# A hybrid decoder layer on one core: sums of weights spread over other blocks, small buffers lent out, state-space outputs one slot later

## The chip, the core and the metric

The kernel runs on one core of a Trainium2 chip. TensorE (PE) does the matrix products, VectorE (DVE) and ScalarE (ACT) the elementwise work, GpSimd (POOL) and SyncE (SP) mostly issue transfers (DMAs); POOL also does a few copies. The metric is device time of one execution in microseconds (us). A profile is one execution recorded by the hardware profiler; its times are its own and stand beside the median of unprofiled executions.

## The reference

One inference step of one decoder layer, for a prompt of 1024 positions and 8 sample rows (1032 tokens, width 1024), in float32:

```
z = x @ w_in + b_in                       # -> ssm input (512) | u, v (2 x 512) | gate_a (1024) | gate_b (1024)
y_a = S5 state-space mixer (32 groups of 16 channels, 64 complex states each), GELU, GLU with w_glu
y_b = u * (tril(W_s) LayerNorm(v) + b)    # in chunks of 128 positions
merged = sigmoid(gate_a) * (y_a @ w_branch_a) + sigmoid(gate_b) * (y_b @ w_branch_b)
x1 = LN1(alpha * x + merged @ w_out + b_out)
x2 = LN2(alpha * x1 + relu(x1 @ w_up + b_up)^2 @ w_down + b_down + sigmoid(x1 @ w_pg + b_pg) * (p @ w_ple))
```

Outputs are x2, the final S5 states and the normalised v rows of the samples.

## The kernel before

Activations lie with features on partitions and tokens in the free dimension. Every float32 product is made of three fast products: an operand is split into a high part (a rounded copy, on ScalarE or VectorE) and a low part (the operand less the high part, on VectorE), and TensorE adds high x high, high x low and low x high. `split` (line 105) makes both parts; a class `Stream` (line 150) loads weights into three `raw` tiles and splits them into four `hl` tiles, three blocks ahead. Line 86 (`tt`) and line 83 (`stt`) are the helpers through which nearly all VectorE operations go, so operations are told apart by their tiles.

The order of the work: input projection of the state-space part; 48 slots, in each of which one third of a gate column block is multiplied (24 matmuls, `gate_tile`), and in which the state-space part is placed by hand in a table (`at(slot, function, ...)`, lines 729 to 761); the v and u parts; the GLU; eight merge blocks of 72 matmuls (lines 999 to 1013); the output projection in two passes with LN1; the gate and embedding products (pg, ple); the up-projection in 16 pairs; the down-projection; LN2. A planner (the framework's) turns this program into one fixed instruction order for each engine and each DMA queue: it takes what its model holds for ready, earlier program text first. On the chip every engine and every queue then goes through its list in order and waits at each instruction for what that needs.

State-space part: `ssm_h` (line 648) makes the carried states H on VectorE with the powers er and ei, stored as (power, group); four transfers on SP's queue put H into the tile Hst. `ssm_y` (line 677) makes the outputs of 8 groups: two matmuls each, of which the second reads Hst, three evacuations on ScalarE into Y, and nine stores. `load_u` and `setup_dve` (lines 553 and 478) prepare the next groups.

The up- and down-projection use a scheme with seven products in place of eight (P1 to P7), so the down-projection needs sums of w_down blocks, S1 to S4. They are made ahead, in 16 sets: `sums_in` (line 933) loads four half tiles ds0 to ds3 (called dsum in the profile) on POOL's queue, `sums_out` (line 946) combines them on VectorE and stores four results on POOL's queue. In front of each load, a one-element copy on VectorE (line 942) writes into the tile from a value made at that point of the program, which ties the load to that moment; the copy itself can run only when the tile's last store has landed. One set is loaded at the end of the u part, two in the GLU, one in each of the eight merge blocks, one in the output projection, and the last four in the first pairs of the up-projection. Outside the sets ds0 serves LN1 and LN2, and ds1 the last normalisation.

The up-projection (`up_pair`, line 1302) takes one pair of 128 hidden columns after the other, 168 matmuls each. Its four `hl` tiles are made by `up_prep` (line 1273) from two weight rows: ra (in a raw tile) and rd (tile rawu in a unit, B18 for even pairs, B19 for odd). B18 and B19 hold parts of the ple operand until the ple products are over. The products P6, P7 and P4 add into the PSUM tile of P1, so each needs the evacuation of the one before it. Squared hidden rows hA and hB and their combinations tA and tB go to DRAM (hd) on POOL's queue; tA and tB have one buffer each.

The down-projection reads hidden rows back: `h_load` (line 1414) loads two of them into a row tile (hraw), of which there are four (`rtags`: B18, A8, A9, B19), and `h_prep`/`h_ahead` (lines 1422 and 1442) split them into 23 operand tiles (hop), each with a one-element copy in front that ties it to a product of the last pair. A8 and A9 are hA and hB of the pair before the last.

Of the kernel before, what the change touches and what calls it, by code (L numbers as in the profile page):

```python
# [32 lines left out]
HF = NTOK // 2  # L33
# [24 lines left out]
def hybrid_step_kernel(ctx: ExitStack, tc: tile.TileContext, i, o):  # L58
# [589 lines left out]
    def ssm_h(hf, gh):  # L648
        g8 = slice(8 * hf, 8 * hf + 8)
        Lv = lview(hf)  # L650
        C = Cc[hf]
        if gh == 0:
            stH[hf] = sp.tile([128, 2, 8, HC], F32, tag="H", name="H")
        H = stH[hf]
        Hv = H[:, :, :, 0:NCH].rearrange("p r g (s b) -> p r g s b", b=8)
        ht = tview(0, (4, 16, 8))
        gs = slice(4 * gh, 4 * gh + 4)
        ge = slice(8 * hf + 4 * gh, 8 * hf + 4 * gh + 4)
        shp = [128, 4, 16, 8]
        eb = lambda x: x[:, 0:8, ge].rearrange("p b g -> p g b").unsqueeze(2).to_broadcast(shp)  # L660
        cb = lambda ri: C[:, ri, gs, 0:16].unsqueeze(3).to_broadcast(shp)
        for ri in range(2):
            tt(V, Hv[:, ri, gs], eb(er), cb(ri), ALU.mult)
            tt(V, ht, eb(ei), cb(1 - ri), ALU.mult)
            tt(V, Hv[:, ri, gs], Hv[:, ri, gs], ht, ALU.subtract if ri == 0 else ALU.add)
            tt(V, Hv[:, ri, gs, :, 1:8], Hv[:, ri, gs, :, 1:8], Lv[:, ri, gs, :, 0:7], ALU.add)
        if gh == 0:
            P.tensor_copy(out=H[:, :, :, NCH:HC], in_=h0[:, :, g8, :])
        else:
            Hst = sp.tile([128, 16, HC], F32, tag="Sst", name="Hst")  # L670
            stS[hf] = Hst
            for ri in range(2):
                for g2 in range(2):
                    nc.sync.dma_start(out=Hst[64 * ri:64 * ri + 64, g2::2, :],
                                      in_=H[64 * g2:64 * g2 + 64, ri])
# [21 lines left out]
    setup_dve(0)  # L697

    carry_powers()
    for mp in range(2):  # L700
        up_ = sp.tile([128, 2, NTOK], F32, tag=["Sst", "L"][mp], name="uperm")
        for j in range(2):
            m = 2 * mp + j
            e = P if j else V
            e.tensor_copy(out=up_[:, j, 0:SEQ].rearrange("p (s n j) -> p s n j", s=8, n=8),
                          in_=ubuf[m][:, 0:SEQ].rearrange("p (n s j) -> p s n j", s=8, n=8))
            e.tensor_copy(out=up_[:, j, SEQ:NTOK], in_=ubuf[m][:, SEQ:NTOK])
            nc.sync.dma_start(out=ud[m], in_=up_[:, j, :])
# [32 lines left out]
    at(14, ssm_l3, 0)  # L741
    at(16, ssm_h, 0, 0)
    at(17, ssm_h, 0, 1)
    at(22, ssm_y, 0)
    at(22, load_u, 2)
    at(23, ssm_y, 1)
    at(23, load_u, 3)
    at(23, setup_dve, 2)
    at(26, setup_pe, 2)
    at(26, setup_dve, 3)  # L750
    at(28, ssm_S, 2)
# [5 lines left out]
    at(37, ssm_l3, 1)  # L757
    at(39, ssm_h, 1, 0)
    at(40, ssm_h, 1, 1)
    at(45, ssm_y, 2)  # L760
    at(46, ssm_y, 3)
    for slot in range(48):
        for f in plan.get(slot, []):
            f()
# [165 lines left out]
    quad = []  # L930
    nq = [0]

    def sums_in(after):

        if nq[0] == 16:
            return
        n = nq[0]
        mp, kh, g = n // 4, n // 2 % 2, n % 2
        nq[0] += 1
        ts_ = [bpool.tile([128, HF], F32, tag=f"ds{t}", name="dsum")[:, 0:512] for t in range(4)]  # L940
        for t, m, j in ((0, mp + 4, 0), (1, mp + 4, 1), (2, mp, 0), (3, mp, 1)):
            V.tensor_copy(out=ts_[t][:, 0:1], in_=after)  # L942
            dn_load(ts_[t], m, j, kh, (g,), nc.gpsimd)
        quad.append((n, ts_))

# [23 lines left out]
    for m in range(4):  # L969
        if m % 2 == 0:  # L970
            w = W("glu", m // 2)
        ps = mm_full([wsl(w, 4 * (m % 2) + k) for k in range(4)], yhl)
        sg = unit(f"T{m % 2}", name="sg")
        S.activation(out=f3(sg), in_=fv(ps), func=AF.Sigmoid, bias=col("b_glu", m))
        tt(V, sg, sg, yt[m], ALU.mult)
        a, b = unit(f"B{8 + m}", F32R, name=f"yah{m}"), unit(f"A{12 + m}", F32R, name=f"yal{m}")
        split(a, b, sg)
        ya.append((a, b))
        split(yb[m][0], yb[m][1], ubt[m])
        if m % 2:  # L980
            sums_out(sg[:, 0:1])
            sums_in(sg[:, 0:1])


    mtags = ["A8", "A9", "A10", "A11", "B0", "B1", "B2", "B3", "B4", "B5", "B6", "B7",
# [13 lines left out]
    for m in range(8):  # L999
        w = W("pab", m)  # L1000
        if m < 7:
            load_gate(m + 1)
        sa, sb = gl.pop(m)
        psB = mm_full([wsl(w, 4 + k) for k in range(4)], yb)
        tt(V, f3(sb), fv(psB), f3(sb), ALU.mult)
        psA = mm_full([wsl(w, k) for k in range(4)], ya)
        tt(V, f3(sa), fv(psA), f3(sa), ALU.mult)
        tt(V, sa, sa, sb, ALU.add)
        a, b = unit(mtags[2 * m], F32R, name=f"mgh{m}"), unit(mtags[2 * m + 1], F32R, name=f"mgl{m}")
        split(a, b, sa)  # L1010
        mg.append((a, b))
        sums_out(sa[:, 0:1])
        sums_in(sa[:, 0:1])

    half = lambda p_: slice(p_ * HF, (p_ + 1) * HF)
    quarter = lambda j: slice(j * QT, (j + 1) * QT)
# [153 lines left out]
    for j, (p_, m) in enumerate(passes):  # L1170
        w = W("out", p_, m)
        load_xr(j + 2)
        sl = half(p_)
        xr = xrs.pop(j)[:, 0:HF]
        S.activation(out=xr, in_=xr, func=AF.Identity, scale=ALPHA, bias=col("b_out", m))
        ps = region2()
        mm_half(ps, [wsl(w, k) for k in range(KD)], [(a[:, sl], b[:, sl]) for a, b in mg])
        tt(V, h2(pre[m][:, sl]), rv(ps), h2(xr), ALU.add)
        if m == 1:
            tt(V, ssum[:, sl], pre[0][:, sl], pre[1][:, sl], ALU.add)  # L1180
        elif m > 1:
            tt(V, ssum[:, sl], ssum[:, sl], pre[m][:, sl], ALU.add)
        if p_ == 0 and m == 7:
            lnx = bpool.tile([128, HF], F32, tag="ds0", name="lnx")
            lnq.add(ln_half(pre, 0, ssum, tmpu, lnx, "ln1_g", "ln1_b", x1_split))
        if p_ == 1:
            lnq.pull(1)
        elif m in (2, 5):
            sums_out(pre[m][:, 0:1])
            if m == 2:  # L1190
                sums_in(pre[m][:, 0:1])


    lnq.drain()
# [78 lines left out]
    def up_prep(n):  # L1273

        p, t = n // 4, n % 4
        if t == 0:
            ra, rb, rc = (raw_() for _ in range(3))
            rd = unit(free[8 + p % 2], F32, [128, 1024], name="rawu")
            upr[p] = (ra, rb, rc, rd)
            nc.sync.dma_start(out=ra, in_=i["w_up"][p])  # L1280
            nc.sync.dma_start(out=rd, in_=i["w_up"][p + NP])
        ra, rb, rc, rd = upr[p]
        if t == 1:
            tt(V, rb[:, D5], rd[:, C5], rd[:, D5], ALU.add)
            tt(V, rb[:, C5], rb[:, D5], ra[:, C5], ALU.subtract)
        elif t == 2:
            tt(V, rc[:, C5], ra[:, C5], rd[:, C5], ALU.subtract)
            tt(V, rc[:, D5], ra[:, D5], rb[:, C5], ALU.subtract)
        w = hl_()
        c = D5 if t == 3 else slice(0, 1024)  # L1290
        split(w[:, 0, c], w[:, 1, c], (ra, rb, rc, rd)[t][:, c])
        wq[n] = w

    def up_ahead(n):
# [7 lines left out]
    def up_pair(p):  # L1302
# [11 lines left out]
        ps = {"P1": a, "P6": a, "P7": a, "P4": a, "P5": c, "P3": c, "P2": b}  # L1314
        last = p == NP - 1
        if last:
            for n in range(4):
                h_load(n)
        for nm, t, cs_ in UPO:
            up_ahead(4 * p + t + 3)  # L1320
# [8 lines left out]
            elif nm == "P5":  # L1329
                S.activation(out=h2(p5), in_=r_, func=AF.Copy)  # L1330
                if last:
                    h_ahead(11, p5[:, 0:1])
            elif nm == "P6":
                S.activation(out=h2(u2s), in_=r_, func=AF.Copy)
                if last:
                    h_ahead(7, u2s[:, 0:1])
            elif nm == "P2":
                stt(V, h2(hA[:, 0]), r_, b1, h2(p1s), ALU.add, ALU.add)
                stt(V, hA[:, 0], hA[:, 0], 0.0, hA[:, 0], ALU.max, ALU.mult)
                put(0, 1, hA[:, 0:1])  # L1340
                if last:
                    h_ahead(3, hA[:, 0, 0:1])
            elif nm == "P7":
                stt(V, h2(hB[:, 1]), r_, b2, h2(p5), ALU.add, ALU.add)
                S.activation(out=hB[:, 1], in_=hB[:, 1], func=AF.Relu)
                S.activation(out=hB[:, 1], in_=hB[:, 1], func=AF.Square)
                if last:
                    h_ahead(13, hB[:, 1, 0:1])
            elif nm == "P3":
                stt(V, h2(hA[:, 1]), r_, b1, h2(u2s), ALU.add, ALU.add)  # L1350
                S.activation(out=hA[:, 1], in_=hA[:, 1], func=AF.Relu)
                S.activation(out=hA[:, 1], in_=hA[:, 1], func=AF.Square)
            else:
                S.activation(out=h2(hB[:, 0]), in_=r_, func=AF.Relu, bias=b2)
                S.activation(out=hB[:, 0], in_=hB[:, 0], func=AF.Square)
# [13 lines left out]
    DNO = ["P1", "P2", "P6", "P7", "P4", "P5", "P3"]  # L1369

    rtags = [free[8], free[2], free[3], free[9]]
    tagof = {id(u): t_ for t_, u in last_of.items()}
    lasts = [tagof[id(u)] for n in ("11", "21", "T2", "T1", "T3", "22", "T4") for u in xq[n]]
    NH = 23
# [39 lines left out]
    def h_load(n):  # L1414

        if n >= 56 or n in hraw:
            return
        r_ = unit(rtags[n % 4], F32, [128, 2, HF], name="hraw")
        nc.sync.dma_start(out=r_, in_=hd[n % 8][HD[PROD[DNO[n // 8]]]].rearrange("s p n -> p s n"))
        hraw[n] = r_  # L1420

    def h_prep(n, after=None):
        if n >= 112:
# [2 lines left out]
        u = unit(ntags[n % NH], F32R, [128, 2, HF], name="hop")  # L1426
        if after is not None:
            V.tensor_copy(out=u[:, 0, 0:1], in_=after)
        src = hraw[n // 2][:, n % 2]
        if n % 5 == 4:  # L1430
            V.tensor_copy(out=u[:, 0, :], in_=src)
        else:
# [2 lines left out]
        hop[n] = (u[:, 0, :], u[:, 1, :])  # L1435
        if n % 2:
            hraw.pop(n // 2)
            for j in range(1, 4):
                if n > 15 or n // 2 + j < 8:
                    h_load(n // 2 + j)  # L1440

# [74 lines left out]

    for p in range(NP):
        up_pair(p)
        u = last_of[ptags[0]][:, 0, 0:1]
        sums_out(u)  # L1520
        sums_in(u)
    assert nq[0] == 16 and not quad

    def sum_(ms, sl, first):
# [231 lines left out]
```

## Time and profile before

| | before |
|---|---|
| median of 3 runs | 1407.98 us (1406.32 to 1411.58) |
| profiled execution | 1411.36 us, span from first to last instruction 1409.4 us |
| PE busy | 1365.3 us (97%), 10302 matmuls |
| DVE busy | 923.2 us (65%) |
| ACT busy | 503.2 us (36%) |
| POOL busy | 200.2 us (14%) |
| mean granted TensorE clock | 0.985 |
| chain that ended last | PE 74%, DVE 12%, DMA 8%, issue 3% |

How to read it: an engine's busy time counts its instructions, not its waiting at semaphores. The granted clock is TensorE's, as a share of full speed (2.4 GHz; its lower level is 1.2 GHz, 0.50). The chain follows the end of the program back from instruction to what released it. A wait is put down to the instruction that came last before it ended.

### The profile page before, as it was taken

The numbers are of one execution on the slowest core, as the hardware profiler recorded it, in microseconds if no ns is written. First come the engines' busy times: TensorE is split into PE (matmuls) and PEld (weight loads), VectorE is DVE, ScalarE is ACT, GpSimd is POOL, SyncE is SP. The second block draws the span as 40 slices with busy tenths as digits, with TensorE's granted clock in tenths as the row PEclk, the third lists the DMA queues.
The fourth block names the chain that finished last, engine by engine and source line by source line (L and its number), as shares of the span: only waits on it lengthen the run. The fifth ranks groups of instructions, "written<-read, shape, count | busy, mean of one in ns | idle before, by whom it ended". The sixth has DMA issues, their size and how long they took to land.

```text
span 1409.4 us, 25105 instructions
## 1 busy us (share of the span) xinstructions
PE 1365.3 (97%) x10302; PEld 1355.4 (96%) x10302; DVE 923.2 (65%) x1631; ACT 503.2 (36%) x696; POOL 200.2 (14%) x318
## 2 busy tenths in 40 slices
PE   9999899999999989999999999999999999999995
PEld 8999899999999879999989999999999999999995
DVE  8929348315787666897777675556557555566857
ACT  3231121133241122464224344344445432343423
POOL 0310310102523331000002320111010000000000
PEclk9999999999999989999999999999999999999998
DMA  7572573541157777432335753453469755665421
GB/s 255 145 186 86 142 173 88 152 138 46 60 196 284 266 271 255 131 125 90 109 133 182 236 195 133 165 160 117 139 222 312 269 194 179 208 211 181 144 97 60
DMA packets 100291, 237.21 MB, mean 168 GB/s; under 512 B 11448, under 2 KB 35912, under 8 KB 100176
## 3 DMA queue, kind: packets, MB, share of 16 engines
q1 hardware_dynamic: 72960, 160.10, 36.0%
q0 software_dynamic: 22128, 72.09, 14.6%
q10 hardware_dynamic: 5088, 3.42, 1.1%
q8 instruction: 81, 1.33, 0.4%
q14 instruction: 34, 0.28, 0.1%
HBM read 160.72 MB, written 68.16 MB: 162 GB/s over the span
## 4 chain that ended last, share of the span: by engine, by line
PE 74%; DVE 12%; DMA 8%; issue 3%; POOL 2%; ACT 1%; SPq 0%; ACTq 0%; DVEq 0%; POOLq 0%
PE q L1134 34%; PE q L1476 19%; PE big L146 5%; DVE tb L86 3%; PE big L123 2%; PE big L125 2%; PE big L124 2%; DMA dsum<-w_down 2%; DVE hl L86 1%; DMA S4d<-dsum 1%; DVE H L86 1%; DMA L<-Sst 1%; PE q L1455 1%; PE q L1456 1%; PE q L1457 1%
## 5 line engine op out<-in xcount | busy, mean ns | idle before, releaser
L86 DVE TENSOR_TENSOR hl<-raw,hl 128x1024 fp32r<-128x1024 f32 (+1 forms) x173 | 210.8, 1221 | 193.0 <-ACT hl L109 192.7
L1476 PE MATMUL q<-hop,hl 128*128 128x258 f32 x2304 | 277.6, 283 | 0.0
L1476 PEld LDWEIGHTS q<-hop,hl 128*128 128x128 f32 x2304 | 277.1, 190 | 0.1
L109 ACT ACTIVATE hl<-raw 128x1024 fp32r<-128x1024 f32 x171 | 180.4, 1056 | 232.2 <-PE q L1476 114.7
L1134 PE MATMUL q<-xb,hl 128*128 128x258 f32 x1920 | 238.0, 283 | 0.0
L1134 PEld LDWEIGHTS q<-xb,hl 128*128 128x128 f32 x1920 | 233.8, 189 | 0.1
L1134 PE MATMUL q<-xT,hl 128*128 128x258 f32 x1536 | 195.8, 288 | 8.0 <-DVE hB L83 4.5
L1134 PEld LDWEIGHTS q<-xT,hl 128*128 128x128 f32 x1536 | 192.5, 195 | 8.6 <-DVE hB L83 4.9
L123 PE MATMUL big<-xh,hl 128*128 128x344 f32 x512 | 165.9, 324 | 1.0 <-ACT uab L296 1.0
L125 PE MATMUL big<-xh,hl 128*128 128x344 f32 x512 | 163.7, 320 | 0.0
L124 PE MATMUL big<-xl,hl 128*128 128x344 f32 x512 | 163.5, 319 | 0.0
L123 PEld LDWEIGHTS big<-xh,hl 128*128 128x128 f32 x512 | 96.2, 188 | 2.0 <-ACT uab L296 1.3
L125 PEld LDWEIGHTS big<-xh,hl 128*128 128x128 f32 x512 | 96.2, 188 | 0.0
L124 PEld LDWEIGHTS big<-xl,hl 128*128 128x128 f32 x512 | 96.2, 188 | 0.0
L1134 PE MATMUL q<-mgh,hl 128*128 128x258 f32 x512 | 84.9, 288 | 4.9 <-DVE dsum L942 4.9
L1134 PEld LDWEIGHTS q<-mgh,hl 128*128 128x128 f32 x512 | 72.3, 193 | 5.3 <-issue 5.2
L86 DVE TENSOR_TENSOR hop<-hraw,hop 128x516 fp32r<-128x516 f32 x112 | 71.7, 691 | 7.7 <-ACT hop L1433 7.4
L1433 ACT ACTIVATE hop<-hraw 128x516 fp32r<-128x516 f32 x90 | 53.6, 628 | 32.8 <-DMA hraw<-hd 25.6
L925 POOL DMA_DIRECT2D dsum<-w_down x48 | 25.8, 540 | 217.0 <-DVE dsum L942 216.5
L719 ACT ACTIVATE sg<-big,vec 128x1032 f32<-128x1032 f32 x16 | 18.0, 1124 | 95.5 <-issue 55.7
L1134 PE MATMUL q<-mgl,hl 128*128 128x258 f32 x256 | 52.1, 285 | 0.0
L83 DVE SCALAR_TENSOR_TENSOR hA<-q,vec,pu 128x516 f32<-128x516 f32 x32 | 24.1, 754 | 38.5 <-issue 22.3
(355 smaller groups left out, 2032.8 us busy)
## 6 DMA issues: line engine op xcount, KB each, us to landing
hraw<-hd SPq DMA_DIRECT2D x56, 516.0 KB, 5.2
dsum<-w_down POOLq DMA_DIRECT2D x48, 256.0 KB, 4.3
gd<-sg SPq DMA_DIRECT2D x16, 516.0 KB, 2.9
hd<-tA POOLq DMA_DIRECT2D x16, 516.0 KB, 3.7
hd<-hB POOLq DMA_DIRECT2D x16, 516.0 KB, 6.2
hd<-tB POOLq DMA_DIRECT2D x16, 516.0 KB, 7.0
raw<-w_gate SPq DMA_DIRECT2D x16, 512.0 KB, 4.7
raw<-w_out SPq DMA_DIRECT2D x16, 512.0 KB, 5.8
```

Source lines behind the costliest of these rows:

```text
L83: eng.scalar_tensor_tensor(out=out, in0=in0, scalar=sc, in1=in1, op0=op0, op1=op1)
L86: eng.tensor_tensor(out=out, in0=a, in1=b, op=op)
L109: S.activation(out=hi, in_=src, func=AF.Copy)
L123: T.matmul(out, wh, xh[:, sl], start=(start and k == 0), stop=False)
L124: T.matmul(out, wh, xl[:, sl], start=False, stop=False)
L125: T.matmul(out, wl, xh[:, sl], start=False, stop=(stop and k == last))
L146: T.matmul(ps[:, t, 0:TT], w_, x_[:, t * TT:(t + 1) * TT], start=st_, stop=sp_)
L719: S.activation(out=f3(sg), in_=fv(ps), func=AF.Sigmoid, bias=col("b_ga" if m < 8 else "b_gb", m % 8))
L925: eng.dma_start(out=r_[:, 512 * k:512 * k + 512], in_=i["w_down"][(2 * n + g) * 4 + m // 2][:, (m % 2) * 512:(m % 2) * 512 + 512])
L1134: T.matmul(ps[:, j, 0:QT], w_, x_[:, j * QT:(j + 1) * QT], start=st_, stop=sp_, skip_group_check=True)
L1433: S.activation(out=u[:, 0, :], in_=src, func=AF.Copy)
L1476: T.matmul(ps[:, j, 0:QT], w_, x_[:, quarter(j)], start=st_, stop=sp_, skip_group_check=True)
```

## The change

Five edits. The products of `ssm_h` read er and ei from copies stored as (group, power). The state-space outputs, and what stood in their slots, come one slot later. The tying copies in `sums_in` go, save for the first set, and the merge makes sums in every second block, so that four sets fewer are loaded ahead of the up-projection, whose pairs 0 to 7 (before: 0 to 3) load one each. The first pair's rd is loaded as two halves into ds1 and ds2. Of the first eight row tiles of the down-projection four (numbers 0, 1, 5 and 6) are loaded as two halves each into ds0 to ds3, five in place of four are asked for at the start of the last pair, and the preparations `h_ahead` stand one product later.

```diff
-        eb = lambda x: x[:, 0:8, ge].rearrange("p b g -> p g b").unsqueeze(2).to_broadcast(shp)
+        eb = lambda x: x[:, ge, :].unsqueeze(2).to_broadcast(shp)
...
-            tt(V, Hv[:, ri, gs], eb(er), cb(ri), ALU.mult)
-            tt(V, ht, eb(ei), cb(1 - ri), ALU.mult)
+            tt(V, Hv[:, ri, gs], eb(ert), cb(ri), ALU.mult)
+            tt(V, ht, eb(eit), cb(1 - ri), ALU.mult)
...
+    ert = sp.tile([128, 16, 8], F32, tag="ert", name="ert")
+    eit = sp.tile([128, 16, 8], F32, tag="eit", name="eit")
+    for dst, src in ((ert, er), (eit, ei)):
+        V.tensor_copy(out=dst, in_=src[:, 0:8, :].rearrange("p b g -> p g b"))
...
-    at(22, ssm_y, 0)
-    at(22, load_u, 2)
-    at(23, ssm_y, 1)
-    at(23, load_u, 3)
-    at(23, setup_dve, 2)
+    at(23, ssm_y, 0)
+    at(23, load_u, 2)
+    at(24, ssm_y, 1)
+    at(24, load_u, 3)
+    at(24, setup_dve, 2)
...
-    at(45, ssm_y, 2)
-    at(46, ssm_y, 3)
+    at(46, ssm_y, 2)
+    at(47, ssm_y, 3)
...
-    def sums_in(after):
+    def sums_in(after=None):
...
-            V.tensor_copy(out=ts_[t][:, 0:1], in_=after)
+            if after is not None:
+                V.tensor_copy(out=ts_[t][:, 0:1], in_=after)
...
-        sums_out(sa[:, 0:1])
-        sums_in(sa[:, 0:1])
+        if m % 2:
+            sums_out(sa[:, 0:1])
+            sums_in()
...
-            rd = unit(free[8 + p % 2], F32, [128, 1024], name="rawu")
-            upr[p] = (ra, rb, rc, rd)
             nc.sync.dma_start(out=ra, in_=i["w_up"][p])
-            nc.sync.dma_start(out=rd, in_=i["w_up"][p + NP])
+            if p:
+                rd = unit(free[8 + p % 2], F32, [128, 1024], name="rawu")
+                nc.sync.dma_start(out=rd, in_=i["w_up"][p + NP])
+                rd5, rd6 = rd[:, C5], rd[:, D5]
+            else:
+                rd5, rd6 = (bpool.tile([128, HF], F32, tag=f"ds{k}", name="rawu")[:, 0:512]
+                            for k in (1, 2))
+                for r_, c in ((rd5, C5), (rd6, D5)):
+                    nc.sync.dma_start(out=r_, in_=i["w_up"][p + NP][:, c])
...
-            for n in range(4):
+            for n in range(5):
                 h_load(n)
...
                 if last:
-                    h_ahead(11, p5[:, 0:1])
+                    h_ahead(7, p5[:, 0:1])
...
                 if last:
-                    h_ahead(7, u2s[:, 0:1])
+                    h_ahead(3, u2s[:, 0:1])
...
-                if last:
-                    h_ahead(3, hA[:, 0, 0:1])
...
                 if last:
-                    h_ahead(13, hB[:, 1, 0:1])
+                    h_ahead(11, hB[:, 1, 0:1])
...
+                if last:
+                    h_ahead(13, hA[:, 1, 0:1])
...
+    HR = [("ds0", "ds1"), ("ds2", "ds3"), free[8], free[2], free[3],
+          ("ds0", "ds1"), ("ds2", "ds3"), free[9]]
...
-        r_ = unit(rtags[n % 4], F32, [128, 2, HF], name="hraw")
-        nc.sync.dma_start(out=r_, in_=hd[n % 8][HD[PROD[DNO[n // 8]]]].rearrange("s p n -> p s n"))
-        hraw[n] = r_
+        src = hd[n % 8][HD[PROD[DNO[n // 8]]]]
+        tg = HR[n] if n < 8 else rtags[n % 4]
+        if isinstance(tg, tuple):
+            hraw[n] = [bpool.tile([128, HF], F32, tag=t_, name="hraw") for t_ in tg]
+            for k in range(2):
+                nc.sync.dma_start(out=hraw[n][k], in_=src[k])
+        else:
+            r_ = unit(tg, F32, [128, 2, HF], name="hraw")
+            nc.sync.dma_start(out=r_, in_=src.rearrange("s p n -> p s n"))
+            hraw[n] = [r_[:, k] for k in range(2)]
...
-            for j in range(1, 4):
+            for j in range(1, 4 if n > 15 else 5):
...
-        u = last_of[ptags[0]][:, 0, 0:1]
-        sums_out(u)
-        sums_in(u)
+        sums_out(last_of[ptags[0]][:, 0, 0:1])
+        sums_in()
```

## Rows read from the trace of the kernel before

**Rows 1.** Waits of PE: engine, line, releaser; us in total, times, longest.

```profile
PE yps L687 <- DMA Hst<-H: 6.7, 4, 2.9
PE q L1134 <- DVE dsum L942: 4.9, 1, 4.9
PE q L1134 <- DVE hB L83: 4.5, 2, 2.4
PE q L1134 <- ACT hl L109: 3.5, 1, 3.5
PE big L146 <- DVE sb L86: 3.4, 3, 1.9
```

**Rows 2.** Stretches: length, busy us of PE, PEld, DVE, ACT, POOL; PEclk, DMA share, GB/s.

```profile
147.00:157.00 10.00, 6.40 (x37) 6.05 (x36) 6.44 (x9) 1.02 (x2) 1.30 (x1) 0.83 0.88 244
258.00:266.00 8.00, 4.86 (x26) 4.49 (x25) 1.22 (x1) 2.58 (x3) 0.00 (x0) 0.79 1.01 295
460.00:519.00 59.00, 48.90 (x287) 47.04 (x286) 43.07 (x71) 10.20 (x10) 19.91 (x37) 0.91 0.78 274
497.00:501.00 4.00, 4.00 (x18) 4.00 (x17) 1.63 (x5) 0.00 (x0) 2.23 (x5) 0.57 0.56 209
513.00:519.00 6.00, 4.87 (x26) 4.90 (x27) 5.64 (x9) 1.07 (x1) 2.19 (x5) 0.58 0.87 267
733.00:744.00 11.00, 7.50 (x42) 7.29 (x41) 9.58 (x14) 3.88 (x5) 2.12 (x4) 0.69 0.68 232
792.00:798.00 6.00, 3.91 (x20) 3.71 (x19) 4.92 (x7) 3.37 (x5) 0.54 (x1) 0.72 0.22 78
1058.00:1065.00 7.00, 4.61 (x27) 4.40 (x27) 6.75 (x17) 5.62 (x10) 0.00 (x0) 0.76 0.96 333
```

**Rows 3.** The chain of waits, in order of time: start us, us, what.

```profile
148.06 4.21 DMA Hst<-H
...
256.33 5.64 DMA Hst<-H
...
282.00 45.47 PE big L146 x288
...
728.41 5.99 DMA rawu<-w_up
...
784.42 7.10 DMA S4d<-dsum
```

**Rows 4.** Timeline of DVE from 136 to 152: start us, us, instruction.

```profile
136.49 1.05 DVE L86 TENSOR_TENSOR H<-er,C 128x512 f32<-128x512 f32 x1
...
151.15 0.69 DVE L86 TENSOR_TENSOR tb<-bb,pwr 128x512 f32<-128x512 f32 x1
```

**Rows 5.** Timeline of POOL and of DVE, 169 to 180.

```profile
171.86 0.53 POOL L695 DMA_DIRECT2D yd<-Y  x1
...
179.20 0.69 DVE L86 TENSOR_TENSOR mt<-tb,tb 128x512 f32<-128x512 f32 x1
```

**Rows 6.** Timeline of DVE in the merge; in brackets idle before and releaser.

```profile
472.34 0.15 DVE L942 COPY dsum<-sa 128x1 f32<-128x1 f32 x1 [2.11 <-DMA S1d<-dsum]
...
512.75 1.23 DVE L86 TENSOR_TENSOR sa<-big,sa 128x1032 f32<-128x1032 f32 x1
```

**Rows 7.** Who waited for line 958 (the sums' stores): us, times.

```profile
  DVE dsum L942: 40.2, 36
```

**Rows 8.** Stretches of the up-projection, with sums and without.

```profile
800.00:820.00 20.00, 20.00 (x169) 20.00 (x168) 14.50 (x26) 8.86 (x14) 6.43 (x12) 1.00 0.72 251
860.00:880.00 20.00, 20.00 (x169) 20.00 (x168) 11.84 (x17) 8.84 (x14) 2.73 (x4) 1.00 0.44 147
```

**Rows 9.** The stretch ahead of the up-projection.

```profile
710.00:734.00 24.00, 23.96 (x199) 23.75 (x197) 18.04 (x29) 4.21 (x6) 1.57 (x3) 1.00 0.30 107
```

**Rows 10.** Timeline of DVE in the last pair.

```profile
1056.65 0.43 DVE L1431 CAST hop<-hraw 128x516 fp32r<-128x516 f32 x1 [3.35 <-DMA hraw<-hd]
```

**Rows 11.** Line 925's instructions on POOL: ns min/median/max, first and last start.

```profile
L925 POOL DMA_DIRECT2D dsum<-w_down x48: 536/541/578, 393.4 to 811.4; - x48
```

More of the change, by code (lines that the diff above doesn't have):

```diff
@@ L981, in hybrid_step_kernel @@
             sums_out(sg[:, 0:1])
-            sums_in(sg[:, 0:1])
+            sums_in()
     mtags = ["A8", "A9", "A10", "A11", "B0", "B1", "B2", "B3", "B4", "B5", "B6", "B7",
@@ L1190, in hybrid_step_kernel @@
             if m == 2:
-                sums_in(pre[m][:, 0:1])
+                sums_in()
     lnq.drain()
@@ L1277, in up_prep @@
             ra, rb, rc = (raw_() for _ in range(3))
-            rd = unit(free[8 + p % 2], F32, [128, 1024], name="rawu")
-            upr[p] = (ra, rb, rc, rd)
             nc.sync.dma_start(out=ra, in_=i["w_up"][p])
-            nc.sync.dma_start(out=rd, in_=i["w_up"][p + NP])
-        ra, rb, rc, rd = upr[p]
+            if p:
[7 more added lines that the diff above has]
+                    nc.sync.dma_start(out=r_, in_=i["w_up"][p + NP][:, c])
+            upr[p] = (ra, rb, rc, rd5, rd6)
+        ra, rb, rc, rd5, rd6 = upr[p]
         if t == 1:
-            tt(V, rb[:, D5], rd[:, C5], rd[:, D5], ALU.add)
+            tt(V, rb[:, D5], rd5, rd6, ALU.add)
             tt(V, rb[:, C5], rb[:, D5], ra[:, C5], ALU.subtract)
         elif t == 2:
-            tt(V, rc[:, C5], ra[:, C5], rd[:, C5], ALU.subtract)
+            tt(V, rc[:, C5], ra[:, C5], rd5, ALU.subtract)
             tt(V, rc[:, D5], ra[:, D5], rb[:, C5], ALU.subtract)
@@ L1290, in up_prep @@
         c = D5 if t == 3 else slice(0, 1024)
-        split(w[:, 0, c], w[:, 1, c], (ra, rb, rc, rd)[t][:, c])
+        split(w[:, 0, c], w[:, 1, c], rd6 if t == 3 else (ra, rb, rc)[t])
         wq[n] = w
@@ L1428, in h_prep @@
             V.tensor_copy(out=u[:, 0, 0:1], in_=after)
-        src = hraw[n // 2][:, n % 2]
+        src = hraw[n // 2][n % 2]
         if n % 5 == 4:
@@ L1518, in hybrid_step_kernel @@
         up_pair(p)
-        u = last_of[ptags[0]][:, 0, 0:1]
-        sums_out(u)
-        sums_in(u)
+        sums_out(last_of[ptags[0]][:, 0, 0:1])
+        sums_in()
     assert nq[0] == 16 and not quad
```

## The prediction

> **What bounds the kernel now.** I read the page first: TensorE (PE) is busy for 97% of the span, VectorE (DVE) for 65%, and the granted clock leaves full speed in only a few slices. So the time is PE's work plus the places where PE stands still, and only those can be won. The second view, PE's own waits, names what it stands for [rows 1]: the carry rows Hst, the copies and products on VectorE around the dsum tiles, VectorE's evacuations (hB, sb), and ScalarE's split hl. Third, busy time and granted clock stretch by stretch, first in steps of 10 us over the whole span and then closely around each hole [rows 2]. What the reader is to see there: six sites where PE's busy time is below the stretch's length, and a clock below 1.00 behind the hole, which is a few us at the lower level (1.2 GHz), where PE is busy but does half the work. A hole is paid twice. For each site, the idle time and (1 - clock) x length:
>
> A, 147 to 157 (first outputs of the state-space part): 3.6 idle + 1.7 clock = 5.3 us.
> B, 258 to 266 (its second half): 3.1 + 1.7 = 4.8 us.
> C, 460 to 519 (merge blocks): 10.1 idle; clock 0.43 x 4 = 1.7, and 0.42 x 6 less 0.5 that fell on idle time = 2.0; together 13.8 us.
> D, 733 to 744 (start of the up-projection): 3.5 + 0.31 x 11 less 0.5 on idle time = 2.9; together 6.4 us.
> E, 792 to 798 (its third pair): 2.1 + 1.7 = 3.8 us.
> F, 1058 to 1065 (its last pair): 2.4 + 1.7 = 4.1 us.
>
> All six make 38.2 us. The start of the kernel and its tail hold most of the other idle time, and the change touches neither.
>
> **The change, part by part.**
>
> Sites A and B. PE reaches the outputs before the rows Hst have landed. The last transfer lands at 148.06 + 4.21 = 152.3, and in the second half at 256.33 + 5.64 = 262.0 [rows 3]; PE is there at about 147.7 and 257.9. One slot is 24 matmuls; 288 of them take 45.47 us [rows 3], so a slot is 3.8 us, and PE would arrive at 151.5 and 261.7. Alone that leaves 0.8 and 0.3 us. The other edit works on the landing: in each half eight products read er or ei with a step of 16 elements. One takes 1.05 us, and a product of the same 512 elements whose operands lie together or repeat takes 0.69 [rows 4]. The new form, eight elements together, is not in the trace: its bounds are 0.69 and 1.05 (it is no worse than the wide step and no better than the plain form). I take 0.69, which it resembles most: 8 x 0.36 = 2.9 us less on a chain that VectorE worked through without a pause, so the rows land near 149.4 and 259.1 and the wait is gone. At the other bound 1.1 us stay. The two new copies (128 elements, a quarter of the strided product's, so by 1.05 / 4 some 0.3 us each; bounds 0 and 1.05) stand on VectorE in the setup, under gate tiles that don't need them; uncovered they cost at most 2.1. Won: 5.3 + 4.8 = 10.1.
>
> What the move takes along: each output call with three evacuations and nine stores (four on SP's queue, five on POOL's), two load_u (four transfers on SP's queue and six on POOL's each), and setup_dve(2). On both queues they pass one gate tile's store and weight load, which have blocks of slack. The next user of load_u is five slots (19 us) off. The nearest edge is the tile mt, which takes the buffer of the stored Y: Y's last store was issued at 171.86 and mt first written at 179.20 [rows 5]. With a landing like that of Hst, 4.2 us, 2.6 us are left for a shift of 3.8, so mt may come 1.2 us late. PE reads it only behind other products of its slot, so I take 0 (bounds 0 and 1.2).
>
> Site C. The 60 one-element copies that tied a load to a moment go (four of 64 stay). One takes 0.15 us, but VectorE is in order and stands until the tile's last store has landed, as in the 2.11 us before one of them [rows 6]: 36 such waits, 40.2 us of idle VectorE [rows 7]. Queued behind them were the sb and sa products for which PE waited [rows 1]; VectorE paced the merge. A block is 72 matmuls, 11.4 us on PE at 0.158 [rows 3]. Afterwards it has five full-width operations on VectorE of at most 1.23 us [rows 6], 6.2 us, and every second one the sums: 14.50 less 11.84 us of VectorE in a pair of the up-projection with and without them [rows 8], 2.7 us. That is 8.9 at most under 11.4, with no store to wait for. Untied, the loads wait on POOL's queue, with only the next sum's stores behind them. A sum is now read 22 us after the one before; its store and load take some 7.1 and 6.0 us by the slowest rows [rows 3]. So C goes, but for the hand-over to the next stage, whose PSUM tiles take the old ones' place: PE waits for the last sa product, 1.23 us [rows 6] and some 0.15 to be seen. Won: 13.8 - 1.4 = 12.4. Bounds: 0 if VectorE still paces, 13.8.
>
> Site D. The first pair's second weight row waits for B18, which a ple operand holds to the end of the ple products. Its transfer runs from 728.41 for 5.99 us [rows 3]; VectorE's combinations and ScalarE's split follow, and PE stands. In two borrowed dsum halves the row lands long before. The combinations and the split then need spare moments of VectorE ahead of 734: it is busy for 18 of 24 us there [rows 9], and they are some 4 us. P6's other operand comes from instructions with an earlier place in the program, so they don't push it back. Won: 6.4 (0 if the split still comes as late). It costs one more issue on SP, before anything PE waits for.
>
> Site E. VectorE stood in the ties for S4d's store, 784.42 + 7.10 [rows 3], and the evacuation of P7 behind them came late. Without ties: 3.8 won. In return further pairs take sums, 2.7 us of VectorE each, and DMA shares rise from 0.44 to 0.72. A pair that had both sums and ties ran at full PE, with VectorE at 14.5 of 20 us [rows 8], so this costs nothing; if that cover failed, 3.8 a pair as at E.
>
> Site F. In the last pair VectorE stands 3.35 us in a conversion whose row tile has not landed [rows 10], and the evacuation of P7 behind it is late. The borrowed tiles let two row tiles land long before, the third takes B18, and each group of preparations follows a product later. Then VectorE is the edge: from P7's end on it has eight subtractions, four sums and two evacuations of about 0.69 [rows 4], two conversions of 0.43 [rows 10] and four weight splits of 1.23 [rows 6], 15.4 us. The last piece is wanted after P3, P4 and 15/16 of the first down product, 24 + 24 + 90 matmuls of 0.12 us (168 in 20 us [rows 8]), 16.4 us. I leave 1.0 us for that: 3.1 won (bounds 0 and 4.1). The halves cost four more issues on SP, at a time when it waits for stores anyway.
>
> Sum: 5.3 + 4.8 + 12.4 + 6.4 + 3.8 + 3.1 = 35.8 us. The profiled execution took 1411.4, 3.4 more than the median of the runs; it would take 1375.6, and the median 1408.0 - 35.8 = 1372.2. I say 1373.
>
> **The rivals.**
>
> The order moves back. PE's order comes from a planner that fills by modelled readiness, not from the slots alone. If it still puts the outputs where Hst is late, A and B stay: 1383. Against it: the slot sets the priority that it works from.
>
> VectorE still paces. In the merge half of C stays (6.9), or at the start of the up-projection D does (6.4), or F: 1380 with one of them, 1390 with all three. For it: only 6 idle us of VectorE ahead of 734 [rows 9], and F's 15.4 in 16.4.
>
> POOL's queue is the new wait. In the pairs with sums the loads stand on POOL ahead of the next hd stores until the sums' stores have landed. tA and tB have one buffer each, so VectorE would stand before the next pair's tA until its store is out. At E a hold of 7.1 us cost PE 3.8, so about 3.3 were covered. Eight sets are stored inside the up-projection. Eight holds must cost 39.6 / 8 = 5.0 each, a hold of 8.3 us, to eat the 35.8 and E's 3.8; a hold of 10 (a store of 7.1 and a put of 3) would cost 8 x 6.7 = 54, less E's 3.8 that is counted as won: 1373 + 3.8 + 54 = 1431, slower than before. It decides from 8.3 us. Against it: a pair leaves tA most of its 20 us, and POOL is busy for 6.4 of them [rows 8].
>
> POOL's issues are held up. An issue took 0.54 us and never over 0.58 [rows 11], with VectorE 72% busy beside it [rows 8]; twelve of them a pair are those 6.4 us. Should each take over 1.7, POOL itself would pace the pairs; at 3 us eight pairs would take 36 us in place of 20, some 130 us more: about 1500. The Trainium skill ("SBUF — State Buffer", section "SBUF: two separate sides") has a rule for it: VectorE's fast one-input copies lock GpSimd out of the port with which it writes its transfers' descriptors, and 620 ns become 3100. No row here shows that, and the sums move to pairs whose VectorE work has two inputs.
>
> The holes turn up one slot or one block further on, and nothing is won: 1401 to 1411.
>
> **How the numbers follow.** Forecast 0.58, order moved back 0.12, VectorE paces 0.15, POOL's queue 0.06, POOL's issues 0.02, nothing won 0.07. Under half a per cent, 7 us, a measurement can't tell a change from none. So faster is 0.58 + 0.12 + 0.15 = 0.85, the same 0.07, slower 0.06 + 0.02 = 0.08. The forecast's own range is 1366 (all six sites, and a few us between executions) to 1380; with the next two cases it reaches 1399, which leaves 0.15 out.
>
> **What would show it.** Right: no PE wait for Hst; products of er's copy at 0.69; merge blocks 11.4 us apart on VectorE; PE at work from 728 on without a hole; VectorE idle before no dsum copy; a clock of 1.00 from 30 us to the tail. Wrong: a hole of 2 us or more behind another releaser at one of the sites, VectorE idle for a dsum load, or tA's writes late behind POOL's stores. A time above 1400 would refute the sum as a whole.

## The result, and the profile after

The changed kernel takes 1374.32 us in the median (1374.12 to 1375.93), the kernel before beside it 1409.78 (1406.32 to 1415.45): a ratio of 0.9747, 95% interval 0.9712 to 0.9782. The forecast was 1373. The time came out as worked out; but the reason given for the largest term (site C) did not hold, as the experiments show.

The page of the changed kernel (busy time, then two rows of the 40 slices) has TensorE busy for 98% and a clock at full speed up to the tail (in stretches of 10 us the granted clock is 1.00 up to 1360 us):

```profile
PE 1350.6 (98%) x10302; PEld 1342.0 (98%) x10302; DVE 908.8 (66%) x1573; ACT 502.7 (37%) x696; POOL 200.0 (15%) x318
...
PE   8999999999999999999999999999999999999995
...
PEclk9999999999999999999999999999999999999998
```

All of PE's waits that the view still lists (us in total, times, longest):

```profile
PE big L306 <- DVE hl L86: 1.7, 1, 1.7
PE q L1140 <- ACT hl L109: 1.4, 1, 1.4
PE wps L248 <- DVE ones L245: 1.1, 1, 1.1
PE big L123 <- ACT uab L296: 1.0, 1, 1.0
PE big L874 <- POOL vt L86: 1.0, 1, 1.0
PE big L146 <- DVE sgt L92: 0.5, 1, 0.5
```

None of the five waits of [rows 1] is there in its old size: Hst, dsum, hB and sb are gone, and hl at line 1134 (1140 now) is 1.4 us where it was 3.5, and at another place. The other five were there before: four at the same length, that at line 306 with 0.8 us. The stretches that answer to [rows 2] (length; busy PE, PEld, DVE, ACT, POOL; clock, DMA share, GB/s): sites A, B, C with its hand-over, D, E, F:

```profile
147.00:157.00 10.00, 10.00 (x74) 10.00 (x73) 4.04 (x6) 1.42 (x3) 2.32 (x4) 1.00 0.73 208
253.00:263.00 10.00, 10.00 (x73) 9.93 (x72) 1.23 (x1) 3.49 (x5) 1.23 (x3) 1.00 0.97 275
400.00:490.00 90.00, 90.00 (x574) 90.00 (x573) 57.51 (x64) 18.05 (x17) 18.28 (x34) 1.00 0.66 231
490.00:500.00 10.00, 8.58 (x68) 8.33 (x67) 8.07 (x11) 4.73 (x6) 1.63 (x3) 1.00 0.41 138
704.00:720.00 16.00, 16.00 (x135) 16.00 (x135) 14.10 (x21) 5.07 (x8) 1.08 (x2) 1.00 0.47 166
760.00:820.00 60.00, 60.00 (x502) 60.00 (x501) 43.56 (x67) 27.12 (x39) 20.14 (x35) 1.00 0.73 248
1018.00:1038.00 20.00, 20.00 (x169) 20.00 (x168) 19.50 (x41) 14.69 (x24) 2.16 (x3) 1.00 0.98 340
```

PE is without a hole at all six, but for the 1.42 us at the hand-over. VectorE's timeline (start, us, instruction, in brackets idle before and releaser) shows what replaced the products of [rows 4] and the waits of [rows 6]:

```profile
132.65 0.69 DVE L86 TENSOR_TENSOR H<-ert,C 128x512 f32<-128x512 f32 x1
...
434.94 1.23 DVE L86 TENSOR_TENSOR sa<-big,sa 128x1032 f32<-128x1032 f32 x1 [2.38 <-PE big L146]
446.27 1.23 DVE L86 TENSOR_TENSOR sa<-big,sa 128x1032 f32<-128x1032 f32 x1 [4.31 <-PE big L146]
```

The products of er take 0.69 us; the merge's sa products come 11.33 us apart, and now VectorE waits for PE, 2.4 us in a block with sums and 4.3 in one without. The standing moved to POOL, where it costs nothing: its waits for the stores ahead of the loads, and the issues themselves (ns min/median/max), which are as long as in [rows 11]:

```profile
POOL dsum L929 <- DMA S3d<-dsum: 29.1, 11, 4.4
```
```profile
L929 POOL DMA_DIRECT2D dsum<-w_down x48: 536/541/578, 384.0 to 859.5; - x48
```

### The profile page after: what moved, and what is told of

Same layout as the page of the kernel before. It is cut to its first block, busy times and chain, and to the rows that moved or that the text cites. A ratio compares the mean times of both kernels' runs of the same rounds, so it can differ in the third digit from the quotient of the medians.

```text
span 1372.5 us, 25043 instructions
## 1 busy us (share of the span) xinstructions
PE 1350.6 (98%) x10302; PEld 1342.0 (98%) x10302; DVE 908.8 (66%) x1573; ACT 502.7 (37%) x696; POOL 200.0 (15%) x318
## 4 chain that ended last, share of the span: by engine, by line
PE 88%; DVE 6%; DMA 3%; issue 1%; ACT 1%; POOL 1%; SPq 1%; ACTq 0%; DVEq 0%
PE q L1140 39%; PE q L1498 19%; PE big L146 11%; PE big L123 4%; PE big L124 4%; PE big L125 4%; DVE tb L86 1%; PE q L1477 1%; PE q L1478 1%; PE q L1479 1%; POOL vt L86 1%; DVE hl L86 1%; DMA L<-Sst 1%; PE big L306 1%; PE sps L581 1%
## 5 line engine op out<-in xcount | busy, mean ns | idle before, releaser
L1140 PE MATMUL q<-xT,hl 128*128 128x258 f32 x1536 | 190.0, 283 | 0.0
L1140 PEld LDWEIGHTS q<-xT,hl 128*128 128x128 f32 x1536 | 187.1, 190 | 0.0
```

The costliest lines, as they stand in the source:

```text
L1140: T.matmul(ps[:, j, 0:QT], w_, x_[:, j * QT:(j + 1) * QT], start=st_, stop=sp_, skip_group_check=True)
```

## Experiments

Times are medians; the changed kernel is at 1374.3, the kernel before, run on the same chip as each experiment, at 1407.5 to 1410.1. A difference of 1.5 to 2 us is thus no larger than that between chips, and is read from the holes in the trace rather than from the time. All but two experiments start from the changed kernel. The diffs show the main lines of each edit; "..." marks what is left out.

**Sites A and B: old slots.**

```diff
-    at(23, ssm_y, 0)
...
-    at(24, ssm_y, 1)
...
+    at(22, ssm_y, 0)
...
+    at(23, ssm_y, 1)
...
-    at(46, ssm_y, 2)
-    at(47, ssm_y, 3)
+    at(45, ssm_y, 2)
+    at(46, ssm_y, 3)
```

> The changed kernel with the state-space outputs, their loads and the setup that follows back in their old slots; the copies of er and ei stay. Theory (both edits are needed; slot 3.8 us): PE comes to the outputs at 148.3 and 253.5, the last rows land at about 149.7 to 150 and 256 to 257; holes of 1.5 and 3 us, 4.5 together, and 1.7 us of lower clock behind the longer or behind each: 1379 to 1382. Rival 1 (the copies alone would have done): no hole, 1374. Rival 2 (short holes don't lower the clock): 1378.5 with a clock of 1.00 behind both.

Measured: 1376.41, 2.1 more. PE's timeline:

```profile
150.34 0.47 PE L687 MATMUL yps<-Hst,O 128*128 128x136 f32 x2 [0.70 <-DMA Hst<-H]
...
255.44 0.50 PE L687 MATMUL yps<-Hst,O 128*128 128x136 f32 x2 [0.94 <-DMA Hst<-H]
```

That is under the 1379 to 1382 expected: the rows landed sooner than I had worked out, the holes are 0.7 and 0.9, and the clock stayed at 1.00 behind both (rival 2 on the clock).

**Sites A and B: no copies.**

```diff
-            tt(V, Hv[:, ri, gs], eb(ert), cb(ri), ALU.mult)
...
+            tt(V, Hv[:, ri, gs], eb(er), cb(ri), ALU.mult)
...
```

> The changed kernel without the copies of er and ei; the products read er and ei with their wide step again, the outputs stay one slot later. Theory (both edits are needed): the products take 1.05 us again, the rows land 2.9 us later, at about 152.8 where PE comes at 152.1, and at 259 to 260 where it comes at 257.3: holes of 0.7 and 2 us, and 1.7 of lower clock behind the second: 1376 to 1379. Rival (the slot alone would have done): 1374, no wait of PE for the rows.

Measured: 1375.85, 1.5 more. A lost 0.04 us of PE, B 0.59 + 0.70, with a clock of 1.00. So with either edit alone each hole is under a microsecond.

**Sites A and B: both undone.**

```diff
-            tt(V, Hv[:, ri, gs], eb(ert), cb(ri), ALU.mult)
...
+            tt(V, Hv[:, ri, gs], eb(er), cb(ri), ALU.mult)
...
-    at(23, ssm_y, 0)
...
+    at(22, ssm_y, 0)
...
```

> The changed kernel with both edits of sites A and B undone: old slots, and no copies of er and ei. One of them undone cost 2.1 and 1.5 us, with holes of at most 0.9 us each and a clock of 1.00 behind them. Theory (holes add up, and once they are long the clock falls behind them too): the holes of the kernel before come back, 3.6 and 3.1 us with 1.7 of lower clock behind each: 10.1, 1384.4. Rival (each edit has its own worth): 2.1 + 1.5 = 3.6, 1378.

Measured: 1384.21, 9.9 more, interval of the ratio to before 0.9822 to 0.9849. The two stretches:

```profile
147.00:157.00 10.00, 6.27 (x36) 5.92 (x35) 6.67 (x10) 0.91 (x2) 1.27 (x1) 0.83 0.90 245
258.00:268.00 10.00, 6.85 (x40) 6.48 (x39) 1.23 (x1) 3.48 (x5) 0.00 (x0) 0.83 0.88 270
```

3.7 and 3.2 idle and 0.17 x 10 = 1.7 of clock behind each: 10.3, where the kernel before had 10.1. The two edits share one gain: either takes most of it (the later slot 8.4, the copies 7.8 of 9.9), and their separate worths, 2.1 and 1.5, don't add up to it.

**Site C: ties back, sums in every second block.**

```diff
-            if after is not None:
-                V.tensor_copy(out=ts_[t][:, 0:1], in_=after)
+            V.tensor_copy(out=ts_[t][:, 0:1], in_=after)
...
-            sums_in()
+            sums_in(sa[:, 0:1])
...
```

> Against the changed kernel (1374.3 us) only the one-element copies that tie each load of the sums to a moment come back; the sums stay in every second merge block. Theory (the ties were what VectorE stood in): in the merge VectorE stands again until a tile's store has landed, but in half of the blocks, so half of site C's 13.8 us comes back, 6.9, and site E's 3.8; together 10.7, 1385 us. Since eight pairs of the up-projection take sums now where four did, up to four more pairs may pay 3.8 each: 1385 to 1400. Copies with idle VectorE of 1 us and more ahead of them in the trace. Rival (it was the number of sums in the merge that VectorE could not carry): no loss, 1374 to 1377.

Measured: 1373.85, no loss: the rival. VectorE stood in the ties again, for 38.9 us in all, and PE lost nothing by it. VectorE's waits, and the merge's stretch of the same kernel:

```profile
DVE dsum L946 <- DMA S3d<-dsum: 20.0, 11, 3.6
DVE dsum L946 <- DMA S2d<-dsum: 10.2, 13, 2.1
DVE dsum L946 <- DMA S4d<-dsum: 6.8, 8, 2.0
DVE dsum L946 <- DMA S1d<-dsum: 1.9, 4, 0.6
```
```profile
400.00:490.00 90.00, 90.00 (x574) 90.00 (x573) 59.53 (x81) 18.11 (x18) 18.47 (x35) 1.00 0.66 230
```

So 40 us of VectorE's standing [rows 7] was no measure of what PE lost. But the ties had less to hold in the merge, as half of its sums are gone: of the 38.9 us only 13.6 fall between 400 and 525 us, where 21.7 of the 40.2 fell before. This run alone does not part the ties from the number of sums; the next ones do.

**Site C: the kernel before, only the ties removed.**

```diff
-            V.tensor_copy(out=ts_[t][:, 0:1], in_=after)
```

> The kernel before with one edit alone: the 60 ties go, nothing else changes; the sums stay in every merge block and in four pairs. Theory (the ties held VectorE): sites C and E go, 12.4 + 3.8 = 16.2 us less: 1409.8 - 16.2 = 1393.6; A, B, D and F stay with their holes. Rival (fewer sums in the merge are needed as well): half of C stays, 1400. Second rival (site D was partly VectorE's lateness from the ties): D shrinks too, 1390.

Measured: 1404.62, ratio 0.9970 (0.9956 to 0.9984), more than the theory and both rivals gave. C stayed whole: in its stretch PE stands still for 60 - 49.35 = 10.7 us, where 10.1 were [rows 2], at the same clock of 0.91. PE's waits for the merge's evacuations are 7.0 and 5.7 us:

```profile
460.00:520.00 60.00, 49.35 (x297) 48.84 (x296) 38.02 (x49) 10.39 (x11) 19.93 (x38) 0.91 0.73 258
```
```profile
PE big L146 <- DVE sb L86: 7.0, 3, 4.9
...
PE q L1133 <- DVE sa L86: 5.7, 1, 5.7
```

VectorE's timeline shows where it stands instead, and POOL's beside it what is late:

```profile
471.48 0.75 DVE L83 SCALAR_TENSOR_TENSOR dsum<-dsum,tie 128x512 f32<-128x512 f32 x1 [7.79 <-DMA dsum<-w_down]
...
473.89 1.23 DVE L86 TENSOR_TENSOR sb<-big,sb 128x1032 f32<-128x1032 f32 x1
```
```profile
456.04 0.54 POOL L957 DMA_DIRECT2D S1d<-dsum  x1 [4.59 <-DVE dsum L83]
...
463.11 2.13 POOL L925 DMA_DIRECT2D dsum<-w_down  x4 [2.32 <-DMA S3d<-dsum]
472.53 0.54 POOL L957 DMA_DIRECT2D S1d<-dsum  x1 [7.29 <-DVE dsum L83]
```

One set of four buffers goes round: sums, stores, the stores' landing, four loads, their landing, the next sums. From S1's store to the next is 472.53 - 456.04 = 16.5 us here (11.6 to 16.5 in the blocks from 428 us on; 11.7 to 13.9 in the kernel before), and a block is 11.3. VectorE, in order, stands for the end of the round; in the kernel before it stood in the ties for the stores, here ahead of the sum for the loads, and sb waits behind either. The 4.8 us that this run did win lie elsewhere: E's hole is gone (PE is busy for 15.00 of the 15 us from 785), D's is 1.85 where it was 3.5, and the clock stayed at 1.00 at F.

**Site C: sums in every block, no ties.**

```diff
-        if m % 2:
-            sums_out(sa[:, 0:1])
-            sums_in()
+        sums_out(sa[:, 0:1])
+        sums_in()
```

> The changed kernel with the sums in every merge block, as in the kernel before, but without ties. Theory (ties): VectorE has 6.2 us of evacuations and 2.7 us of sums a block, 8.9 under PE's 11.4, so the time stays: 1373 to 1377; the blocks stay 11.3 us apart. Store and load of a set take up to 7.1 + 6.0 = 13.1 us, over one block's 11.4, so VectorE may stand up to 1.7 us a block for a load, which the spare 2.5 covers. Rival (VectorE paces the merge as soon as each block has a sum, since it stands for loads): blocks of 12 to 13 us and half of site C back, about 6.9: 1381.

Measured: 1388.62, 14.3 more, twice what even the rival gave. The holes in PE's timeline:

```profile
435.26 0.74 PE L146 MATMUL big<-ybh,hl 128*128 128x344 f32 x3 [1.00 <-DVE sb L86]
448.39 0.71 PE L146 MATMUL big<-ybh,hl 128*128 128x344 f32 x3 [1.52 <-DVE sb L86]
461.87 0.76 PE L146 MATMUL big<-ybh,hl 128*128 128x344 f32 x3 [1.92 <-DVE sb L86]
...
501.88 0.77 PE L1139 MATMUL q<-mgh,hl 128*128 128x258 f32 x2 [3.95 <-DVE sa L86]
```

My expectation had 13.1 us for store and load against a block's 11.4 and let VectorE's spare 2.5 us absorb the rest. It can't: time that VectorE stands in order ahead of sb is not spare.

**Site C: the kernel before, only the sums in every second block.**

```diff
-        sums_out(sa[:, 0:1])
-        sums_in(sa[:, 0:1])
+        if m % 2:
+            sums_out(sa[:, 0:1])
+            sums_in(sa[:, 0:1])
```

> The kernel before with one edit alone: the sums in every second merge block; all ties stay, and so does everything else. The theory has changed: the prediction held the ties for what paced VectorE, but with ties and half of the sums nothing was lost, and without ties and all of the sums site C stayed. New theory (one set of four buffers is stored and loaded again in 13 to 17 us, more than the 11.4 us of a block; VectorE stands for the end of that round, in the ties or ahead of the next sum alike): with 22.7 us a round C goes but for the hand-over, 12.4 us less: 1409.4 - 12.4 = 1397; sites A, B and F stay, E stays or goes as one slow store of S4d falls, so 1393 to 1397. Rival (the ties hold VectorE even so): half of C stays, 1403 or more.

Measured: 1392.09, ratio 0.9888 (0.9874 to 0.9901), 15.4 less than the kernel before beside it; of the profiled spans, 1409.4 - 1390.5 = 18.9 less. The expectation (1393 to 1397) started from that span; the kernel before took 1411.36 when it was profiled, 3.8 more than its median here, which accounts for what lies between 18.9 and 15.4. Ties and all, C has no hole left but the 1.4 of the hand-over, and E none (PE is busy for 30.00 of the 30 us from 770). The merge's stretch:

```profile
410.00:500.00 90.00, 90.00 (x574) 90.00 (x573) 60.47 (x82) 18.05 (x17) 19.30 (x36) 1.00 0.66 232
```

This one edit made C's 12.4 us, and with it E and a part of D and F: the hole at D was 2.98 with 1.7 of clock (4.7 where 6.4 were); at F it was longer than before, 2.69 for 2.39, but the clock stayed at 1.00 (2.7 where 4.1 were). 12.4 + 3.8 + 1.7 + 1.4 = 19.3 against the 18.9.

**Site C: sums in seven blocks, two sets of buffers.**

```diff
-        if m % 2:
+        if m < 7:
...
+        if n in (3, 5, 7):
+            ts_ = [unit(t_, name="dsum")[:, 0:512] for t_ in ("T0", "T1", "B15", "B16")]
...
```

Left out: one more set is loaded ahead of the merge, and the sums take the older of the two sets.

> The changed kernel with sums in seven of the eight merge blocks, as many as made 1388.6 us of it before, but with a second set of four buffers (units that are free in the merge) that takes turns with the first, so that a set again has two blocks, 22.7 us, for its sums, stores and next loads. Theory (not the number of sums, but the round of one set of buffers, 13 to 17 us, is what VectorE stood for): no loss, blocks 11.3 us apart, no VectorE wait for a dsum load of 2 us or more: 1374 to 1377. Rival 1 (each block with sums costs, since VectorE's share or the transfers' traffic pace it): 1385 to 1389. Rival 2 (POOL, which issues loads and stores in order, is now the round): holes in some blocks, 1378 to 1384.

Measured: 1373.90, no loss. VectorE's waits for loads, and the merge's stretch:

```profile
DVE dsum L83 <- DMA dsum<-w_dl: 1.6, 1, 1.6
DVE dsum L86 <- DMA dsum<-w_down: 1.0, 1, 1.0
```
```profile
400.00:490.00 90.00, 90.00 (x574) 90.00 (x573) 68.91 (x88) 18.79 (x18) 33.13 (x62) 1.00 0.89 307
```

VectorE does 68.9 us of work in 90, the transfers run at 307 GB/s, and PE has no hole. So neither the number of sums nor the traffic paced the merge, but the round of one set. With the two runs that start from the kernel before, that settles C.

**The hand-over behind the merge: PSUM tiles in turned order.**

```diff
     load_gate(0)
+    big()
     for m in range(8):
```

> The changed kernel with the two PSUM tiles of the merge in turned order (one is taken and not used ahead of the merge), so that the last product's tile is the other one. Theory (the 1.4 us at the hand-over are PE's wait for the PSUM tile that the last sa product reads, since the output projection's first tile lies in its place): the wait goes, 1374.3 - 1.4 = 1373. Rival (the new tiles wait for all of the old pool, or PE waits for ScalarE's split of a weight, as the wait is put down): no change.

Measured: 1373.99, and the hole is still 1.42:

```profile
491.68 1.23 DVE L86 TENSOR_TENSOR sa<-big,sa 128x1032 f32<-128x1032 f32 x1 [4.29 <-PE big L146]
492.43 1.04 ACT L109 ACTIVATE hl<-raw 128x1024 fp32r<-128x1024 f32 x1
...
493.06 0.48 PE L1141 MATMUL q<-mgh,hl 128*128 128x258 f32 x2 [1.42 <-DVE sa L86]
```

PE starts 0.15 us after the sa product's end (492.91) and ahead of the split's (493.47), so it waits for VectorE's last read of the old tiles, whichever tile that is. That the new tiles wait for all of the old ones fits; it was not tried by itself.

**Site D: the first pair's second row back in its unit.**

```diff
-            if p:
+            if True:
                 rd = unit(free[8 + p % 2], F32, [128, 1024], name="rawu")
```

> The changed kernel with the first pair's second weight row back in its unit buffer, which a ple operand holds to the end of the ple products. Theory (site D is this transfer): the row lands some 6 us after the ple products' end, VectorE's combinations and ScalarE's split follow, and PE stands about 3.5 us and loses 2.9 to the clock: 6.4, 1380.7 us. Rival (VectorE, held up by the ties and sums before, made half of the hole): a hole under 2 us, 1375 to 1377.

Measured: 1377.82 (1376.2 to 1379.1), 3.5 more, between the theory's 1380.7 and the rival; the profiled span is 1.9 longer. PE's timeline:

```profile
712.52 1.22 PE L1140 MATMUL q<-xT,hl 128*128 128x258 f32 x8 [1.89 <-ACT hl L109]
714.12 7.95 PE L1140 MATMUL q<-xT,hl 128*128 128x258 f32 x64 [0.37 <-DVE hl L86]
```

2.3 us of hole at full clock, where the kernel before had 3.5 and a lower clock. Here the row's transfers landed within 4.4 us and no sum's load was issued beside them; in the kernel before four were and the row took 5.99 [rows 3]. In two further traces it is the same: with such loads (sums in every second block) 5.5 us and a hole of 2.98; without (only the ties removed) 4.3 and 1.85. POOL's issues of that set, in the kernel before, then with sums in every second block, then with only the ties removed (the last of four; the others went at 562 to 565 us):

```profile
732.42 2.15 POOL L925 DMA_DIRECT2D dsum<-w_down  x4 [172.97 <-DVE dsum L942]
```
```profile
720.16 2.15 POOL L925 DMA_DIRECT2D dsum<-w_down  x4 [174.23 <-DVE dsum L942]
```
```profile
639.51 0.54 POOL L925 DMA_DIRECT2D dsum<-w_down  x1 [74.29 <-DVE lnt L86]
```

So it was the ties that held these loads until the row was under way; without ties they go out as their buffers come free. Holes of 2.98 and 3.50 with the meeting and of 1.85 and 2.3 without it put its price at 0.7 to 1.7 us. That is argued from four traces: no run moved these loads alone.

**Site F: the last pair as before.** Borrowed tiles, the fifth early load and the order of preparations undone.

```diff
-        tg = HR[n] if n < 8 else rtags[n % 4]
+        tg = rtags[n % 4]
```

> The changed kernel with the last pair as it was before: no borrowed row tiles, four loads ahead, each group of preparations after the product it followed then. Theory (site F is VectorE standing for a row tile): VectorE idle some 3.4 us ahead of a conversion, a hole of PE of 2.4 us and 1.7 of lower clock: 1378.4. Rival (what came before it, the sums of the pairs, made VectorE late): no hole, 1374 to 1375.

Measured: 1375.78, 1.5 more, between the two. VectorE stood 2.38 us for the row tile (3.35 in [rows 10]), PE 1.35 for hB, and the clock stayed at 1.00.

**Site F: only the order back.** Each group of preparations after its old product, as this one.

```diff
-                    h_ahead(7, p5[:, 0:1])
+                    h_ahead(11, p5[:, 0:1])
```

> The changed kernel with the borrowed row tiles kept, but each group of preparations in the last pair after the product it followed before. Theory of the prediction (the tiles win most of F, the order keeps VectorE's evacuations ahead of preparations): the preparations no longer wait for a row tile, but stand ahead of the evacuation of P7 again; VectorE has 15.4 us for 16.4, so a hole of 0 to 1.5 us: 1374 to 1376. Rival (the order did it): the hole of 2.4 us and its clock come back, 1378.

Measured: 1374.31, no loss, no hole. The tiles (with the fifth early load, which stayed) made F's gain, the order none that can be measured.

## Why the prediction was right, point by point

**A and B: right, 10.1 against 9.9.** Of its steps, the products went from 1.05 to 0.69 as taken, and the two copies took 0.27 each. PE came to the first outputs at 152.1, near the 151.5 worked out, and at 257.3 (the 261.7 worked out, less the 5.3 won at A, is 256.4). That the slot alone leaves 0.8 and 0.3 was off by 0.8 and 1.0: 0.04 and 1.29 were measured. What the prediction didn't see is how little the second of the two edits adds once one is there.

**C: the size was right, the step failed.** "Queued behind them were the sb and sa products for which PE waited [rows 1]; VectorE paced the merge" was put on the ties, by their 36 waits and 40.2 us. The ties alone, removed or put back, changed nothing at C. What the prediction added as a remark, that a sum is now read 22 us after the one before, was the whole cause: the old loop asked one set of buffers for a round of 11.7 to 13.9 us in each block of 11.3. The ties showed the store half of that round; the load half hardly showed in the trace of before (VectorE waited 6.3 us in all for the sums' loads there), since it ran on beside the next block's work. With the ties gone it is the half that VectorE stands for, 30.4 us in eight waits (19.1 + 11.3, only the ties removed). That the sum came out is luck: the edit that the step credited won nothing at C, and the one that did it all stood beside it in the change, with no more than a remark. The 1.4 at the hand-over was right (1.42 measured) and PE does wait for the last sa product; but it does so whichever old tile that product reads, so the place of a single tile is not the reason.

**D and F: won whole, but not by their own edits alone.** Undone in the changed kernel they cost 3.5 and 1.5 us, not 6.4 and 4.1. At D the rest goes, as argued above, with the ties, without which four loads of sums no longer meet the row's transfer, and with a clock that no longer fell; the prediction put all 6.4 on the row's place. At F the clock stayed at 1.00 in every run but the kernel before itself. What took F's hole from 2.39 to the 1.35 with its edits undone stays open: neither the ties' removal alone (2.56) nor the fewer sums alone (2.69) did it. F's leftover of 1.0 didn't appear: PE was busy for 20.00 of 20 us, with VectorE at 19.5, so the edge that I had worked out was there and held.

**E: right in place, too general in cause.** The hole went with the ties removed, but also with all ties back. In the kernel before VectorE stood 2.95 + 2.03 + 1.88 = 6.9 us in one set's ties there; in the changed kernel with ties the longest such stand is 2.20 + 0.85 + 0.96 = 4.0, and no hole followed. So it reads as one late set of stores, whose last took 7.10 us [rows 3]; no run delayed such a set by itself.

**The rivals.** POOL's queue took over the wait for the stores, at most 4.4 us at a time against the 8.3 from which it would decide. POOL's issues stayed at 0.54 us with VectorE 66% busy, and none took over 0.58. The rule of the Trainium skill ("SBUF — State Buffer", section "SBUF: two separate sides"), by which a transfer that GpSimd issues takes some 3100 ns in place of 620 beside a copy on VectorE, doesn't show in these issues; no run was made to load VectorE with such copies. VectorE doesn't pace the merge even with sums in seven blocks.

## What to carry to other kernels

An in-order engine that stands for a transfer shows one half of a buffer's round; take that wait away and it stands for the other half. Work out the whole round (last use, store, landing, load, landing, next use) against the period in which the loop asks for it, and then lengthen the period or add a second set. And put each of two edits back by itself before crediting either: two that remove the same hole are each worth most of it alone and little beside the other (here 7.8 and 8.4 of 9.9 us, against 2.1 and 1.5).

## What I had not expected of the hardware

A hole was not always paid twice. The clock stayed at 1.00 behind holes of 0.70 and 0.94 (old slots), 1.35 (last pair back) and even 2.56 and 2.69 at F in the kernel before with only the ties removed and with the sums in every second block. The latter:

```profile
1040.00:1050.00 10.00, 7.31 (x61) 7.11 (x60) 9.91 (x22) 8.83 (x15) 0.00 (x0) 1.00 0.95 323
1050.00:1060.00 10.00, 10.00 (x85) 10.00 (x84) 8.04 (x20) 3.42 (x5) 2.16 (x3) 1.00 1.02 355
```

It fell to the lower level (1.2 GHz) for some us behind holes of 1.85 (D, only the ties removed) and 2.39 (F, kernel before). The former:

```profile
736.00:743.00 7.00, 5.14 (x31) 4.94 (x30) 7.00 (x11) 3.58 (x4) 0.00 (x0) 0.76 0.32 97
```

So the length of one hole didn't decide it here; what did stays open. Where it fell, the loss was mostly 1.7 us (0.24 x 7 in this row, 0.17 x 10 at A and at B with both edits undone), and 2.9 at D in the kernel before.
